# Eight of eleven steps by seven products in the first pair of column blocks of each half

## The chip, the cores and the metric

The kernel runs on one core of a Trainium2 chip. The metric is the device time of one execution in microseconds. Before the change it is 1205.45 us, the median of three runs (1204.93 to 1205.78).

The core's engines run side by side and wait for each other by semaphores. TensorE (PE) multiplies matrices into PSUM, where this kernel keeps eight tiles of 128 x 512 float32 numbers. VectorE (DVE) and ScalarE (ACT) do elementwise work. GpSimd (POOL) does some more and issues DMAs, and SyncE (SP) issues most DMAs. The program holds one order of instructions for each engine.

## The reference

It is one decoder layer over 16 meta tokens and 256 tokens of width 2048: eight retention heads and four mLSTM heads behind one input projection, an output projection, and then a causal ConvFFN and a last norm. The change lies in the ConvFFN and the last norm:

```python
u = rmsnorm(h, norm_ffn)
up = causal_dwconv(u @ w_up, ffn_conv_w, ffn_conv_b)   # 2048 -> 2 * 5632
gate, val = jnp.split(up, [FFN_DIM], axis=-1)
h = h + (jax.nn.silu(gate) * val) @ w_down             # 5632 -> 2048
return rmsnorm(h, norm_final)[:, N_META:]
```

## The kernel before

**Precision.** Every float32 operand of a large product is split into a high part, which ScalarE rounds (`whi`, a CAST), and a low part, which VectorE subtracts (`wlo`). One product of two tiles is then three matmuls: high by high, low by high, high by low.

**Halves.** The hidden width of 5632 is 44 blocks of 128. They are done in two halves of 22 blocks. A half has an up stage, which makes its 22 gated blocks (tiles `gt`), and a down stage, which multiplies them by `w_down` into the 256 x 2048 output. The down stage runs over the output's four column blocks of 512 in two pairs: `b = 0` (blocks 0 and 1), then `b = 2` (blocks 2 and 3). Within a pair it runs over 11 steps `q`; a step takes two of the 22 hidden blocks.

**Plain steps and steps by seven.** In a pair and a step there are 2 x 2 blocks of activations (two hidden blocks, two halves of the tokens) and 2 x 2 blocks of weights (two hidden blocks, two column blocks). A plain step (`product`, L814) does the eight block products, 24 matmuls of 128 x 512. It loads two weight blocks of 128 x 1024 (`load_step`, L910, and `load_w`, L113), and each wants one cast on ScalarE (L119) and one subtraction on VectorE (L121). A step by seven (`seven`, L830) is Winograd's form of Strassen's scheme: seven block products, 21 matmuls, from sums of blocks. It loads weights into a half of the old `hT` tile (`raw`, two of them in turn), makes three differences of weights on VectorE (`ta` and `tb`, L842 and L843), and splits seven blocks in four pieces (L853, through `split`, L764 and L766). The matmuls of a step by seven are L857, L858 and L860. One weight sum of it is made ahead in the up stage by `Early` (L600): GpSimd's queue fetches three weight blocks, VectorE does two operations on them (L616, L617), and GpSimd's queue writes the sum to HBM (`kept`), from where `seven` reads it. `pace` (L609) is a one-column operation of GpSimd's that holds such a fetch back.

**Which steps.** `FAST` lists seven steps, 1, 2, 3, 5, 6, 7 and 8; the other four are `PLAIN`. All pairs do the seven, save the last one (half 1, `b = 2`), where `BOTH`, the steps 7 and 8, are plain; for them the block `a21` is kept split as well. The up stage prepares a fast step's activations in 128 x 128 blocks and four sums of them, which GpSimd makes (L802 to L805).

**What ends a pair.** The four plain sums of a pair (PSUM tiles `atps`, in the code `cs`) and the four shared products of the steps by seven (PSUM tiles `mmps`, in the code `ps`) are put together by VectorE: `share` (L878; L883, L884, L888 and L892) and then four additions (L950). Each addition frees one `atps` bank for the next pair, whose first plain products want it.

**Buffers and order.** Weights come into four buffers `wraw`, which `ta` and `tb` use too; `whi` and `wlo` have five buffers each. The order on each engine is written by a scheduler that models the time of each instruction, from the order of the code and its priorities. The names `x_5852` and `x_5851` in its rows are the tile `x5`, on which `share` and the additions work.

**Small tiles.** `ss4`, `pace`, `rest`, `fr0` and `frt` hold sums of squares and scales of the last norm, and one pacing column. They stand in a pool of their own. `par` holds all parameter columns; those named `cw`, 32 columns, are the mLSTM's convolution weights, which nothing reads once the heads are done.

## Time and profile before

| | |
|---|---|
| Median of three runs | 1205.45 us |
| The profiled execution | 1205.27 us |
| Its span, first to last instruction | 1203.4 us |
| TensorE busy | 1194.6 us, 99% of the span |
| VectorE busy | 978.2 us, 81% |
| ScalarE busy | 704.2 us, 59% |
| GpSimd busy | 156.2 us, 13% |
| Matmuls | 8956 |

The profiled execution took 1.9 us more than its span, which is the time around the first and the last instruction. Busy time says how long an engine had an instruction in work, not how well it used it: matmuls overlap, so the time that one costs is read from one start to the next. The same holds for VectorE, whose instructions overlap by a little. In half 0 the down stage's first pair begins at 717.9 us and its second at 773.65 us, in half 1 at 1082.5 us and 1138.1 us.

### The profile page before, as it was taken

The numbers are of one execution on the slowest core, as the hardware profiler recorded it, in microseconds if no ns is written. First come the engines' busy times: TensorE is split into PE (matmuls) and PEld (weight loads), VectorE is DVE, ScalarE is ACT, GpSimd is POOL, SyncE is SP. The second block draws the span as 40 slices with busy tenths as digits, with TensorE's granted clock in tenths as the row PEclk, the third lists the DMA queues.
The fourth block names the chain that finished last, engine by engine and source line by source line (L and its number), as shares of the span: only waits on it lengthen the run. The fifth ranks groups of instructions, "written<-read, shape, count | busy, mean of one in ns | idle before, by whom it ended". The sixth has DMA issues, their size and how long they took to land.

```text
span 1203.4 us, 22768 instructions
## 1 busy us (share of the span) xinstructions
PE 1194.6 (99%) x8956; PEld 1152.1 (96%) x8956; DVE 978.2 (81%) x1458; ACT 704.2 (59%) x952; POOL 156.2 (13%) x210
## 2 busy tenths in 40 slices
PE   9999999999999999999999999999999999999997
PEld 9999999999999999999999998888999999998886
DVE  8868787766775867788989889998788778789997
ACT  8757656655656556555555556565555555556564
POOL 0100001111110311121112100101122112100131
PEclk9999999999999999999999999999999999999999
DMA  7765555566565965766866734658777677755756
GB/s 279 266 215 165 171 181 172 197 182 196 167 193 161 339 212 181 244 215 209 267 211 221 267 136 175 209 211 272 247 260 253 221 244 245 257 178 209 259 167 192
DMA packets 81275, 260.12 MB, mean 216 GB/s; under 512 B 14480, under 2 KB 18704, under 8 KB 81040
## 3 DMA queue, kind: packets, MB, share of 16 engines
q1 hardware_dynamic: 71952, 223.85, 56.3%
q0 software_dynamic: 8640, 33.96, 8.7%
q8 instruction: 70, 1.15, 0.4%
q10 hardware_dynamic: 576, 0.85, 0.2%
q14 instruction: 37, 0.30, 0.1%
HBM read 243.42 MB, written 11.27 MB: 212 GB/s over the span
## 4 chain that ended last, share of the span: by engine, by line
PE 99%; DMA 0%; SPq 0%; DVE 0%; ACT 0%; issue 0%; DVEq 0%; ACTq 0%
PE mmps L128 26%; PE mmps L129 25%; PE mmps L131 25%; PE atps L828 8%; PE mmps L858 2%; PE mmps L860 2%; PE mmps L857 2%; PE atps L858 1%; PE atps L860 1%; PE atps L857 1%; PE atps L380 1%; PE atps L372 0%; DMA wraw<-in_w 0%; PE atps L128 0%; PE atps L381 0%; PE atps L131 0%
## 5 line engine op out<-in xcount | busy, mean ns | idle before, releaser
L119 ACT CAST whi<-wraw 128x1024 fp32r<-128x1024 f32 x352 | 369.0, 1050 | 329.5 <-PE mmps L129 221.7
L121 DVE TENSOR_TENSOR wlo<-wraw,whi 128x1024 fp32r<-128x1024 f32 x352 | 432.2, 1231 | 66.5 <-ACT whi L119 63.0
L128 PE MATMUL mmps<-uh,whi 128*128 128x258 f32 x1408 | 346.1, 283 | 0.0
L129 PE MATMUL mmps<-ul,whi 128*128 128x258 f32 x1408 | 346.0, 283 | 0.0
L128 PEld LDWEIGHTS mmps<-uh,whi 128*128 128x128 f32 x1408 | 267.6, 190 | 0.1
L129 PEld LDWEIGHTS mmps<-ul,whi 128*128 128x128 f32 x1408 | 267.1, 190 | 0.1
L128 PE MATMUL mmps<-xh,whi 128*128 128x272 f32 (+2 forms) x864 | 219.9, 288 | 0.0
L129 PE MATMUL mmps<-xl,whi 128*128 128x272 f32 (+2 forms) x864 | 218.4, 286 | 0.0
L131 PE MATMUL mmps<-uh,wlo 128*128 128x258 f32 x1408 | 196.5, 282 | 0.0
L131 PEld LDWEIGHTS mmps<-uh,wlo 128*128 128x128 f32 x1408 | 179.9, 189 | 0.0
L129 PEld LDWEIGHTS mmps<-xl,whi 128*128 128x128 f32 x864 | 163.0, 189 | 0.0
L128 PEld LDWEIGHTS mmps<-xh,whi 128*128 128x128 f32 x864 | 162.6, 188 | 0.1
L131 PE MATMUL mmps<-xh,wlo 128*128 128x272 f32 (+2 forms) x864 | 126.8, 286 | 0.0
L131 PEld LDWEIGHTS mmps<-xh,wlo 128*128 128x128 f32 x864 | 114.4, 188 | 0.0
L681 DVE TENSOR_TENSOR cu<-mmps,rstd 128x258 f32<-128x258 f32 x88 | 37.4, 425 | 51.9 <-PE mmps L131 51.1
L764 ACT CAST whi<-hT 128x1024 fp32r<-128x1024 f32 x52 | 53.5, 1051 | 28.1 <-PE atps L828 8.4
L766 DVE TENSOR_TENSOR wlo<-hT,whi 128x1024 fp32r<-128x1024 f32 x52 | 62.7, 1229 | 4.9 <-ACT whi L764 3.7
L129 PE MATMUL mmps<-mixl,whi 128*128 128x258 f32 x256 | 63.0, 283 | 0.0
L128 PE MATMUL mmps<-mixh,whi 128*128 128x258 f32 x256 | 62.4, 282 | 0.0
L764 ACT CAST whi<-wraw 128x1024 fp32r<-128x1024 f32 (+1 forms) x52 | 42.9, 836 | 25.8 <-PE mmps L858 6.0
L766 DVE TENSOR_TENSOR wlo<-wraw,whi 128x1024 fp32r<-128x1024 f32 (+1 forms) x52 | 51.3, 1015 | 1.1 <-PE mmps L860 0.2
L828 PE MATMUL atps<-whi,ml 128*128 128x512 f32 (+1 forms) x132 | 50.7, 385 | 0.0
(284 smaller groups left out, 1696.7 us busy)
## 6 DMA issues: line engine op xcount, KB each, us to landing
wraw<-in_wu SPq DMA_DIRECT2D x176, 512.0 KB, 4.4
wraw<-in_wi SPq DMA_DIRECT2D x108, 512.0 KB, 4.1
hT<-in_wd SPq DMA_DIRECT2D x26, 768.0 KB, 4.7
wraw<-in_wd SPq DMA_DIRECT2D x36, 512.0 KB, 5.2
wraw<-in_wo SPq DMA_DIRECT2D x32, 512.0 KB, 4.4
x<-in_wd POOLq DMA_DIRECT2D x13, 768.0 KB, 7.2
hT<-kept SPq DMA_DIRECT2D x26, 256.0 KB, 2.7
hT<-in_wd POOLq DMA_DIRECT2D x8, 768.0 KB, 6.1
```

What stands on the lines that cost most here:

```text
L119: nc.scalar.copy(hi, raw)
L121: nc.vector.tensor_tensor(out=lo, in0=raw, in1=hi.bitcast(F32), op=ALU.subtract)
L128: nc.tensor.matmul(ps, hi[:, k, :], xh(kk), start=kk == first, stop=False)
L129: nc.tensor.matmul(ps, hi[:, k, :], xl(kk), start=False, stop=False)
L131: nc.tensor.matmul(ps, lo[:, k, :], xh(kk), start=False, stop=kk == last)
L681: evacuated = nc.vector.tensor_tensor(out=u, in0=ps[:, :NQ], in1=rstd2, op=ALU.mult)
L764: copied = nc.scalar.copy(hi, x)
L766: return copied, nc.vector.tensor_tensor(out=lo, in0=x, in1=hi.bitcast(F32), op=ALU.subtract)
L828: nc.tensor.matmul(ps, a, m[:, i, cols], start=first and n == 0, stop=seed or last and n == 5, skip_group_check=seeded)
L857: nc.tensor.matmul(o, sh[:, f, m, :], hi[:, i, :], start=begin, stop=False)
L858: nc.tensor.matmul(o, sl[:, f, m, :], hi[:, i, :], start=False, stop=False)
L860: nc.tensor.matmul(o, sh[:, f, m, :], lo[:, i, :], start=False, stop=end)
```

## The change

`FAST` gets an eighth step, 9, so `PLAIN` is left with 0, 4 and 10. A table `SEVEN` says which fast steps go by seven products in which pair: all eight in the first pair of each half, seven in the second pair of half 0 (9 stays plain there), and the same five as before (1, 2, 3, 5 and 6) in the last pair. `BOTH` names by half the steps that are plain in its second pair, and whose `a21` block is kept. `Early` makes two sums more, one in each half. To make room in SBUF, the small tiles of the last norm and `pace` move into columns of `cw`, and the tile `vt` of the up stage has one buffer in place of two.

```diff
-    FAST = [1, 2, 3, 5, 6, 7, 8]
+    FAST = [1, 2, 3, 5, 6, 7, 8, 9]
     PLAIN = [q for q in range(NQD) if q not in FAST]
-    BOTH = FAST[-2:]
+    BOTH = {0: [9], 1: [7, 8, 9]}
+    SEVEN = {(0, 0): FAST, (0, 2): FAST[:-1], (1, 0): FAST, (1, 2): FAST[:-3]}
...
-    ss4 = midp.tile([P, 2, 5], F32, name="ss4")
+    ss4 = pcol("cw", 0, 10).rearrange("p (t i) -> p t i", t=2)
...
-    pace = midp.tile([P, 1], F32, name="pace")
+    pace = pcol("cw", 10)
...
-        o = wk2.tile([P, SEQ], F32, name=name)
+        o = wk2.tile([P, SEQ], F32, name=name, bufs=2 if name == "gt" else 1)
...
-    rest = midp.tile([P, 2], F32, name="rest")
-    r0 = midp.tile([P, 2], F32, name="fr0")
-    rt = midp.tile([P, 2], F32, name="frt")
+    rest, r0, rt = (pcol("cw", 11 + 2 * i, 2) for i in range(3))
...
-        units = [(b, q) for b in (0, 2) for q in FAST if (half, b) != (1, 2) or q not in BOTH]
+        units = [(b, q) for b in (0, 2) for q in SEVEN[half, b]]
...
-            begins = [2 + 4 * i for i in range(9)]
-            homes = 9 * [homes[2]]
+            begins = [2 + 4 * i for i in range(10)]
+            homes = 10 * [homes[2]]
...
-                if half == 1 and q in BOTH:
-                    split(*(a[:, BOTH.index(q), :] for a in a21), e21)
+                if q in BOTH[half]:
+                    split(*(a[BOTH[half].index(q)] for a in a21), e21)
...
-            fast = [q for q in steps if q in FAST and not (final and q in BOTH)]
+            fast = [q for q in steps if q in SEVEN[half, b]]
```

The order moves on VectorE where the first pair of a half ends. These are the rows of before there, in half 0: they begin with the two low parts of the weights of step 9, and end with the first two of the four additions (L950).

```order
L121 TENSOR_TENSOR wlo<-wraw,whi 128x1024 x2
L883 TENSOR_TENSOR x_5852<-mmps,x_5852 128x512
L884 TENSOR_TENSOR x_5852<-mmps,x_5852 128x512
L888 TENSOR_TENSOR x_5852<-x_5852,mmps 128x512
L892 TENSOR_TENSOR x_5852<-x_5852,mmps 128x512
L121 TENSOR_TENSOR wlo<-wraw,whi 128x1024
L842 TENSOR_TENSOR wraw<-hT 128x1024
L121 TENSOR_TENSOR wlo<-wraw,whi 128x1024 x2
L843 TENSOR_TENSOR wraw<-hT 128x512
L950 TENSOR_TENSOR x_5852<-atps,x_5852 128x512
L121 TENSOR_TENSOR wlo<-wraw,whi 128x1024
L950 TENSOR_TENSOR x_5852<-atps,x_5852 128x512
```

The four operations of `share` (L883 to L892) stand together, well ahead of the first addition, and only one difference of the next pair (L842, L843) stands between. The same place in the changed program, where all line numbers are lower by one; the two low parts at the head are those of step 10, for step 9 has none:

```order
L121 TENSOR_TENSOR wlo<-wraw,whi 128x1024 x2
L882 TENSOR_TENSOR x_5851<-mmps,x_5851 128x512
L841 TENSOR_TENSOR wraw<-hT 128x1024
L842 TENSOR_TENSOR wraw<-hT 128x512
L883 TENSOR_TENSOR x_5851<-mmps,x_5851 128x512
L949 TENSOR_TENSOR x_5851<-atps,x_5851 128x512
L121 TENSOR_TENSOR wlo<-wraw,whi 128x1024
L887 TENSOR_TENSOR x_5851<-x_5851,mmps 128x512
L891 TENSOR_TENSOR x_5851<-x_5851,mmps 128x512
L121 TENSOR_TENSOR wlo<-wraw,whi 128x1024
L841 TENSOR_TENSOR wraw<-hT 128x1024
L949 TENSOR_TENSOR x_5851<-atps,x_5851 128x512 x3
```

`share` is now spread out (L882, L883, L887, L891), the first addition stands in the middle of it, and a whole pair of differences for the next pair (L841, L842) and a third wide one (L841) stand ahead of the other three additions. In half 1 the rows of before are those of half 0 but for the last one, which is three additions. Those of the change there, from the first low part of step 10 on:

```order
L121 TENSOR_TENSOR wlo<-wraw,whi 128x1024
L882 TENSOR_TENSOR x_5851<-mmps,x_5851 128x512
L121 TENSOR_TENSOR wlo<-wraw,whi 128x1024
L841 TENSOR_TENSOR wraw<-hT 128x1024
L883 TENSOR_TENSOR x_5851<-mmps,x_5851 128x512
L842 TENSOR_TENSOR wraw<-hT 128x512
L949 TENSOR_TENSOR x_5851<-atps,x_5851 128x512
L887 TENSOR_TENSOR x_5851<-x_5851,mmps 128x512
L891 TENSOR_TENSOR x_5851<-x_5851,mmps 128x512
L121 TENSOR_TENSOR wlo<-wraw,whi 128x1024 x2
L949 TENSOR_TENSOR x_5851<-atps,x_5851 128x512 x3
```

Here the low part of the next pair's first weights (the first of the two at L121 behind L891) stands behind the first addition and both last operations of `share`; in half 0 it stands between the first addition and those.

## Rows read from the trace of the kernel before

**Rows 1.** The page's head: span; busy time, share and instructions of each engine

```profile
span 1203.4 us, 22768 instructions
PE 1194.6 (99%) x8956; PEld 1152.1 (96%) x8956; DVE 978.2 (81%) x1458; ACT 704.2 (59%) x952; POOL 156.2 (13%) x210
```

**Rows 2.** The page's chain that ended last, share of the span by engine

```profile
PE 99%; DMA 0%; SPq 0%; DVE 0%; ACT 0%; issue 0%; DVEq 0%; ACTq 0%
```

**Rows 3.** Busy time of each engine in three stretches; first line names the columns

```profile
core 0: us, PE busy (x) PEld busy (x) DVE busy (x) ACT busy (x) POOL busy (x), PEclk, DMA share, GB/s
717.00:774.00 57.00, 57.00 (x254) 46.68 (x254) 51.25 (x56) 36.32 (x40) 0.19 (x1) 1.00 0.56 203
...
829.00:1082.00 253.00, 253.00 (x2109) 252.82 (x2108) 200.93 (x300) 136.59 (x184) 41.84 (x68) 1.00 0.72 242
1082.00:1138.00 56.00, 56.00 (x249) 46.05 (x248) 52.16 (x58) 37.48 (x42) 1.33 (x2) 1.00 0.65 231
```

**Rows 4.** Timeline, TensorE, first pair of half 0: its begin and end

```profile
start us, us, engine line op out<-in xcount [idle before <-releaser]
717.89 0.39 PE L828 MATMUL atps<-whi,mh 128*128 128x512 f32 x1
718.12 0.39 PE L828 MATMUL atps<-whi,ml 128*128 128x512 f32 x1
...
772.60 1.07 PE L828 MATMUL atps<-wlo,mh 128*128 128x512 f32 x4
773.65 0.47 PE L828 MATMUL atps<-whi,mh 128*128 128x512 f32 x1
```

**Rows 5.** Timeline, VectorE: last steps by seven of that pair, and an addition

```profile
749.34 1.82 DVE L766 TENSOR_TENSOR wlo<-wraw,whi 128x1024 fp32r<-128x1024 f32 x2
751.08 2.35 DVE L766 TENSOR_TENSOR wlo<-hT,whi 128x1024 fp32r<-128x1024 f32 x2
753.35 1.22 DVE L842 TENSOR_TENSOR wraw<-hT 128x1024 f32<-128x1024 f32 x1
754.48 0.68 DVE L843 TENSOR_TENSOR wraw<-hT 128x512 f32<-128x512 f32 x1
755.09 1.82 DVE L766 TENSOR_TENSOR wlo<-wraw,whi 128x1024 fp32r<-128x1024 f32 x2
...
759.09 1.82 DVE L766 TENSOR_TENSOR wlo<-wraw,whi 128x1024 fp32r<-128x1024 f32 x2
...
772.82 0.68 DVE L950 TENSOR_TENSOR x<-atps,x 128x512 f32<-128x512 f32 x1
```

**Rows 6.** Timeline, TensorE: where it uses the piece that VectorE makes from 759.09

```profile
762.75 0.62 PE L860 MATMUL mmps<-wlo,sh 128*128 128x512 f32 x2
```

**Rows 7.** Groups of VectorE instructions by form, 718 to 829 us

```profile
L766 DVE TENSOR_TENSOR wlo<-hT,whi 128x1024 fp32r<-128x1024 f32 x26 | 31.0, 1219 | 1.7 <-ACT whi L764 1.7
L843 DVE TENSOR_TENSOR wraw<-hT 128x512 f32<-128x512 f32 x12 | 8.2, 684 | 0.0
L950 DVE TENSOR_TENSOR x<-atps,x 128x512 f32<-128x512 f32 x5 | 3.3, 684 | 0.0
```

**Rows 8.** Timeline, ScalarE: casts of plain steps' weights and what they waited for

```profile
766.46 1.05 ACT L119 CAST whi<-wraw 128x1024 fp32r<-128x1024 f32 x1 [2.84 <-DMA wraw<-in_wd]
767.73 1.05 ACT L119 CAST whi<-wraw 128x1024 fp32r<-128x1024 f32 x1 [0.22 <-DMA wraw<-in_wd]
...
770.31 1.05 ACT L119 CAST whi<-wraw 128x1024 fp32r<-128x1024 f32 x1 [0.23 <-DMA wraw<-in_wd]
```

**Rows 9.** Timeline, half 1: VectorE at 1118, TensorE at the second pair's begin

```profile
1118.74 1.82 DVE L766 TENSOR_TENSOR wlo<-wraw,whi 128x1024 fp32r<-128x1024 f32 x2
...
1138.13 0.39 PE L828 MATMUL atps<-whi,mh 128*128 128x512 f32 x1
```

**Rows 10.** Groups of VectorE and GpSimd instructions, 480 to 717 us

```profile
L616 DVE TENSOR_TENSOR x<-x 128x512 f32<-128x512 f32 x9 | 6.2, 688 | 4.0 <-DMA x<-in_wd 4.0
...
L804 POOL TENSOR_TENSOR x<-x,gt 128x128 f32<-128x128 f32 x7 | 6.8, 967 | 0.6
```

More of the change, by code (lines that the diff above doesn't have):

```diff
@@ L760, in trunk @@
         sl = midp.tile([P, len(FAST), 7, P], F32R, name="sl")
-        a21 = [midp.tile([P, len(BOTH), P], F32R, name=n) for n in ("a21h", "a21l")]
+        a21 = [[m[:, i, :] for i in range(3)] for m in [midp.tile([P, 3, P], F32R, name=n) for n in ("a21h", "a21l")]]
         def split(hi, lo, x, after=None):
@@ L823, in product @@
                 f = FAST.index(q)
-                ah, al = ([m[:, f, A12 if i else A11, :] if tt == 0 else m[:, f, A22, :] if i else a[:, BOTH.index(q), :] for i in range(2)]
+                ah, al = ([m[:, f, A12 if i else A11, :] if tt == 0 else m[:, f, A22, :] if i else a[BOTH[half].index(q)] for i in range(2)]
                           for m, a in zip((sh, sl), a21))
```

## The prediction

> **What bounds the kernel now.** I read the page's head first: TensorE is busy 99% of the span and VectorE 81% [rows 1]. The chain that ended last agrees: 99% of it is TensorE [rows 2]. So what shortens TensorE's own work shortens the kernel, and what makes TensorE wait lengthens it, with no slack on either side. The stages come next. In the first pair of each down stage TensorE is busy all the time at a granted clock of 1.00, that is 2.4 GHz, but VectorE is busy 51.25 of 57 us in half 0 and 52.16 of 56 us in half 1, 90% and 93%, well over its 81% of the whole [rows 3]. The change adds VectorE work exactly there. The timelines then give the rates. One 128 x 512 matmul follows another after 0.228 us (717.89 to 718.12, and four of them from 772.60 make 773.51); the pair takes 7 x 21 + 4 x 24 = 243 of them, from 717.89 to 773.65, that is 55.76 us or 0.2295 each, with one stall of 0.14 us in it, at 773.51 [rows 4]. Else TensorE keeps its pace throughout.
>
> **What is removed.** A plain step costs TensorE 24 matmuls and a step by seven 21. One step changes its kind in the first pair of half 0 and one in that of half 1; the other pairs keep seven and five. That is 6 matmuls fewer, 6 x 0.2286 = 1.37 us, all on the path that sets the end. The 0.14 us at 773.51 belong to the place that I work out below, so they leave the sum there too. Together 1.51 us can be won at most.
>
> **What is added, on VectorE.** A step by seven costs VectorE four wide operations (1024 columns) and two narrow ones (512). From 749.34 to 755.09 one such step follows another with no idle time, so it takes 5.75 us; in these rows a wide one costs 1.135 us start to start (two from 751.08 to 753.35) and a narrow one 0.60 us (754.48 to 755.09) [rows 5]. The mean durations, 1.219 and 0.684 us, are longer because neighbours overlap [rows 7]. TensorE's share of the step is 21 x 0.2286 = 4.80 us. So in a run of such steps VectorE falls behind by 0.95 us a step, and catches up in plain ones: two wide operations, 2.27 us, against 24 x 0.2286 = 5.49 us. Before, the run is 5, 6, 7, 8, and 9 and 10 are there to catch up. Now 9 belongs to the run, and only 10 is left before the pair's end, where `share` and the four additions come due.
>
> How far ahead is VectorE? The last wide piece of the run in half 0 is made from 759.09 to 760.31; TensorE takes it at 762.75 [rows 5, 6]. That is 2.4 us of lead. Up to 759.09 the change moves nothing in that pair, so I go on from there in the order of the changed program. From there to the second of the four additions stand 11 wide operations (the first piece at 759.09, one difference of step 9 and its three wide pieces, the two low parts of step 10, two wide differences of the next pair, and the two low parts of its first step) and 9 narrow ones (a piece of step 8, the narrow difference and piece of step 9, one narrow difference of the next pair, the four of `share`, and the first addition). 759.09 + 11 x 1.135 + 9 x 0.60 = 776.98; the addition takes 0.684 us [rows 7] and ends at 777.66. On it waits the first product of the next pair into the bank that it empties. TensorE comes there at 773.51 - 3 x 0.2286 + 16 x 0.2286 = 776.48: the pair is three matmuls shorter, and 16 of the next pair stand ahead. The hand-over takes 0.15 us: before, the first addition ran from 772.82 for 0.68 us, and the product that waited for it started at 773.65 [rows 4, 5]. So TensorE waits 777.66 + 0.15 - 776.48 = 1.3 us.
>
> This holds if nothing else delays VectorE on the way. One thing may. Four buffers go round, so the first weight block of the next pair now lands in the one that step 9's wide difference leaves. Before, the block that came three loads behind a run's last wide difference was cast at 766.46 after a wait for its DMA, and that buffer had been free since 760.31: 6.15 us [rows 5, 8]. Now the low part that reads that difference last has four wide and two narrow operations ahead of it: 759.09 + 4 x 1.135 + 2 x 0.60 + 1.22 = 766.05. The cast then starts at 772.2 and ends at 773.25. VectorE's slot for its low part would be 759.09 + 8 x 1.135 + 7 x 0.60 = 772.37, so everything behind slips by 0.9 us. TensorE wants the cast at 772.82 and the low part four matmuls later, and loses 0.45 us at the one and 0.5 at the other; the wait at the addition shrinks as much as it slips and stays 1.3 us. That makes 2.2 us. So half 0 loses 1.3 to 2.2 us.
>
> In half 1 the same place is ordered otherwise. From 1118.74 [rows 9] 11 wide and 7 narrow operations lead to the first addition, at 1135.43, but that one has to wait for its own bank, whose last product starts seven matmuls before the pair's end at 1138.13 - 0.69 = 1137.44 and takes 0.39 us: 1136.23. Behind it stand two operations of `share`, and then the low part that the next pair's fifth matmul wants: 1136.23 + 3 x 0.60 + 1.22 = 1139.25, with the hand-over 1139.4. TensorE comes there at 1137.44 + 4 x 0.2286 = 1138.35 and waits 1.05 us. After that the additions come in time.
>
> **What I cost at nothing.** In the up stages step 9 now wants one split of 128 columns more, four small sums on GpSimd of up to 0.97 us each, and `Early` two VectorE operations of 0.69 us and one more fetch a half [rows 10]. VectorE has 52 us to spare in the 253 us of the second up stage, and GpSimd works 42 of them [rows 3]; TensorE doesn't wait there now. Without that cover it would be some 2 us a half. The one buffer of `vt` is read by a product that ends before the next block pair is half done. The small tiles in `cw` are written and read by the same instructions as before; only their place is new. The tail has no instruction more for it. If a tie to other columns of `par` added waits there, each would cost a hand-over of 0.15 us, for some five operations in a row 0.75 us; a gain I see no reason for.
>
> **The sum.** -1.51 + (1.3 to 2.2) + 1.05 = +0.85 to +1.75 us, in the middle +1.3. On the profiled execution's 1205.27 us that is 1206.6; the median of the runs stands 0.18 us above it, so I predict 1206.8 us. The ends are those of the first half: no delay by the load, or the delay of the row. About 0.2%, 2.4 us, is what a measurement of this kernel can tell from no change, and my forecast lies within it.
>
> **Rivals.**
> - *The gain comes whole* (1205.45 - 1.51 = 1203.9 us). For it speaks that TensorE is the chain and that VectorE's 81% leave room [rows 1, 2]; the lead would have to be 1 to 2 us longer than I count, as it is where a stage's order lets VectorE work ahead. The Trainium skill's "Perfetto Trace Analysis", section "Identifying the Most-Contended Engine", says to find the engine with the highest occupancy and work on that one; by it the change takes work from the right engine and the whole 1.51 us would show. Its measure for TensorE, LDWEIGHTS busy, is 96% here [rows 1], which agrees, but VectorE's 90% in these stages is what the average hides [rows 3].
> - *The loads make it slower* (1209.4 us). Step 9's transfers fall into the burst at the pair's end. Landings there come 1.28 us apart (766.46, 767.73) and casts wait for them [rows 8]. A step by seven fetches 1 MB, twice a plain block, so if it goes ahead of the next pair's weights in one half these are 2 x 1.28 = 2.6 us later, and TensorE with them: 1206.8 + 2.6. It decides from 1.1 us of such delay on, where the bound of 2.4 us over the median is passed. Against it: a block of step 9 can be fetched as soon as step 7 has used its half of `hT`, two steps of 4.80 us earlier.
> - *VectorE's operations don't overlap* (1209.4 us). Had each its full 1.219 or 0.684 us [rows 7], some 0.084 us more, the 20 operations of half 0 would take 1.7 us longer; the 18 of half 1 would take 1.5 us, of which 0.8 are hidden by the wait for the bank, and the three behind it 0.25: 1206.8 + 1.7 + 0.95. The Trainium skill's "VectorE: DVE Perf Modes", section "The DRAIN you can't avoid", says that the next operation doesn't start until the pipe is empty, though it excepts one that isn't held back; by the plain rule this time would come. The trace speaks against it: 1.135 us start to start for operations of 1.22 us [rows 5].
>
> That the step isn't taken off TensorE can't be: the changed program holds six matmuls fewer.
>
> **How the numbers follow.** Forecast 0.48, whole gain 0.26, later loads 0.17, no overlap 0.03, and 0.06 for a shift elsewhere, either way. The forecast and the whole gain lie within 2.4 us, but a gain of 1.5 us with some luck in the order could reach past it (0.04); the slow ones lie beyond. So faster 0.04, same 0.74, slower 0.22. The range goes from 1203.8, the whole gain, to 1208.9, which leaves out the later loads at their full price. The forecast's own range is 1206.3 to 1207.3.
>
> **What would show it.** TensorE's timeline should have 21 matmuls for step 9 in both first pairs. At the begin of the second pair of half 0 a gap of 1 to 2 us should stand before a plain product that waits for an addition of VectorE, and in half 1 one of 1 us before a low part. VectorE should be without idle time for some 20 us ahead of both. If these gaps are not there I am wrong about the lead; if they stand behind a cast that waits for a DMA, the second rival is right; if gaps stand in the up stages or the tail, my noughts are wrong.

## The result, and the profile after

The changed kernel takes 1211.63 us in the median of six runs (1210.63 to 1215.02), the kernel before on the same chip 1205.35 us: a ratio of 1.0058, 95% interval 1.0049 to 1.0068. It is slower by 6.3 us, 0.6%, where I forecast +1.4 and no change that can be told; the measured time lies beyond the upper end of my range, 1208.9. The profiled execution took 1210.63 us, with a span of 1208.7 against 1203.4 us.

The page's head and its chain of waits, which answer to [rows 1, 2]:

```profile
span 1208.7 us, 22809 instructions
PE 1194.6 (99%) x8950; PEld 1148.8 (95%) x8950; DVE 987.2 (82%) x1474; ACT 706.6 (58%) x960; POOL 167.2 (14%) x224
PE 93%; DVE 3%; DMA 2%; issue 1%; ACT 0%; DVEq 0%; SPq 0%; ACTq 0%
```

The six matmuls are gone (8956 to 8950). But the chain, which was TensorE alone, now leads through VectorE and DMAs for 5% of the span. TensorE's timeline says where; these are its rows that begin after idle time in half 0 and half 1 (the bracket says for how long, and what ended it), and the row ahead of the first:

```profile
765.75 0.61 PE L859 MATMUL mmps<-wlo,sh 128*128 128x512 f32 x2
767.28 0.50 PE L827 MATMUL atps<-whi,mh 128*128 128x512 f32 x1 [0.91 <-ACT whi L119]
776.36 0.50 PE L856 MATMUL mmps<-whi,sh 128*128 128x512 f32 x1 [0.22 <-ACT whi L763]
778.75 0.50 PE L827 MATMUL atps<-whi,mh 128*128 128x512 f32 x1 [0.24 <-DVE x L949]
790.29 0.50 PE L856 MATMUL atps<-whi,sh 128*128 128x512 f32 x1 [0.56 <-ACT whi L763]
...
1134.19 0.50 PE L827 MATMUL atps<-whi,mh 128*128 128x512 f32 x1 [0.94 <-ACT whi L119]
1141.40 0.50 PE L827 MATMUL atps<-whi,mh 128*128 128x512 f32 x1 [0.80 <-ACT whi L119]
1143.12 0.73 PE L827 MATMUL atps<-wlo,mh 128*128 128x512 f32 x2 [0.52 <-DVE wlo L121]
1144.55 0.50 PE L856 MATMUL mmps<-whi,sh 128*128 128x512 f32 x1 [0.22 <-ACT whi L763]
1180.39 0.73 PE L859 MATMUL mmps<-wlo,sh 128*128 128x512 f32 x2 [0.62 <-DVE wlo L765]
```

What a wait costs is read start to start: two matmuls from 765.75 would let the next begin at 765.75 + 2 x 0.2286 = 766.21; it began at 767.28, so 1.07 us are lost. Summed in this way over the places that stand out, half 0 lost 1.07 + 0.16 + 0.39 + 0.42 + 0.72 = 2.76 us, half 1 0.14 + 1.11 + 0.96 + 0.69 + 0.39 + 0.78 = 4.07 us. With the 1.37 us won and the 0.14 of before that is +5.3 us, as much as the span grew by. There are no new gaps in the up stages and the tail.

That the sum comes out is partly luck, for it leaves out two things that cancel. It leaves out small losses: 0.27 us in the two matmuls ahead of 775.40, and some 0.1 us each time TensorE starts again behind a wait. With these the waits are 8.4 us. And it leaves out that TensorE's pace changed. In each pair of rows, 50 matmuls lie from the first to the second; before:

```profile
740.09 0.39 PE L828 MATMUL atps<-whi,mh 128*128 128x512 f32 x1
...
751.53 0.39 PE L858 MATMUL mmps<-whi,sl 128*128 128x512 f32 x1
```

After:

```profile
740.14 0.39 PE L827 MATMUL atps<-whi,ml 128*128 128x512 f32 x1
...
751.47 0.39 PE L856 MATMUL atps<-whi,sh 128*128 128x512 f32 x1
```

That is 11.44 us against 11.33, or 0.2288 against 0.2266 us a matmul, at a granted clock of 1.00 in both. The difference runs through both kernels' down stages wherever TensorE doesn't wait. For the some 950 matmuls of this width there it makes about 2.1 us won, an estimate from these rows. So the waits cost more than the 5.3 us by which the span grew: 5.3 + 1.37 + 0.14 + 2.1, some 9 us.

Most of the rows name ScalarE's casts. ScalarE's timeline tells what these waited for; the four of the border in half 0 answer to [rows 8]:

```profile
766.18 1.04 ACT L119 CAST whi<-wraw 128x1024 fp32r<-128x1024 f32 x1 [3.05 <-DMA wraw<-in_wd]
767.65 1.05 ACT L119 CAST whi<-wraw 128x1024 fp32r<-128x1024 f32 x1 [0.42 <-DMA wraw<-in_wd]
...
772.10 1.05 ACT L119 CAST whi<-wraw 128x1024 fp32r<-128x1024 f32 x1 [2.92 <-DMA wraw<-in_wd]
773.36 1.05 ACT L119 CAST whi<-wraw 128x1024 fp32r<-128x1024 f32 x1 [0.21 <-DMA wraw<-in_wd]
```

The first two are step 10's, the others those of the next pair's step 0. VectorE meanwhile did what I had added up from [rows 5], up to 764.84. Then it waited for step 10's casts, 0.60 us at 767.26 and 0.25 us at 768.73, so that the first addition came at 772.81, where the sum gives 771.8. The second began at 778.01. I had worked out 776.98, and 777.9 if the next pair's load delayed VectorE; but the low part of that load, at 773.41, didn't wait.

```profile
759.10 1.22 DVE L765 TENSOR_TENSOR wlo<-wraw,whi 128x1024 fp32r<-128x1024 f32 x1
...
764.84 1.82 DVE L765 TENSOR_TENSOR wlo<-wraw,whi 128x1024 fp32r<-128x1024 f32 x2
767.26 1.23 DVE L121 TENSOR_TENSOR wlo<-wraw,whi 128x1024 fp32r<-128x1024 f32 x1 [0.60 <-ACT whi L119]
...
772.81 0.68 DVE L949 TENSOR_TENSOR x<-atps,x 128x512 f32<-128x512 f32 x1
773.41 1.21 DVE L121 TENSOR_TENSOR wlo<-wraw,whi 128x1024 fp32r<-128x1024 f32 x1
...
778.01 1.88 DVE L949 TENSOR_TENSOR x<-atps,x 128x512 f32<-128x512 f32 x3
```

SP's queue shows when the loads were issued. Before (each pair of `kept` and `in_wd` is the 1 MB of a step by seven, each `wraw` 512 KB of a plain one):

```profile
759.20 0.33 SPq L838 DMA_DIRECT2D hT<-kept  x1
759.59 0.42 SPq L839 DMA_DIRECT2D hT<-in_wd  x1
760.34 4.41 SPq L116 DMA_DIRECT2D wraw<-in_wd  x4
```

After:

```profile
759.21 0.33 SPq L837 DMA_DIRECT2D hT<-kept  x1
759.59 0.41 SPq L838 DMA_DIRECT2D hT<-in_wd  x1
760.34 2.67 SPq L116 DMA_DIRECT2D wraw<-in_wd  x2
764.95 0.33 SPq L837 DMA_DIRECT2D hT<-kept  x1
765.32 0.43 SPq L838 DMA_DIRECT2D hT<-in_wd  x1
766.08 0.93 SPq L116 DMA_DIRECT2D wraw<-in_wd  x2
```

Step 10's weights are issued at 760.34 in both, when VectorE's low part frees their buffer. Before, a plain step lay between the run and step 10; now TensorE wants them right behind the run, and they take 5.74 us (chain of waits). The next pair's weights, issued by 764.75 before, are issued at 766.08. That is when their buffer comes free, for the low part that reads step 9's wide difference ends at 766.06. Just ahead of them in the queue, at 764.95, stands 1 MB of rows of the next pair's step 2 (step 1's are those of 759.21).

### The profile page after: what moved, and what is told of

Its sections match the earlier page's. It is cut to its first block, busy times and chain, and to the rows that moved or that the text cites. A ratio compares the mean times of both kernels' runs of the same rounds, so it can differ in the third digit from the quotient of the medians.

```text
span 1208.7 us, 22809 instructions
## 1 busy us (share of the span) xinstructions
PE 1194.6 (99%) x8950; PEld 1148.8 (95%) x8950; DVE 987.2 (82%) x1474; ACT 706.6 (58%) x960; POOL 167.2 (14%) x224
## 4 chain that ended last, share of the span: by engine, by line
PE 93%; DVE 3%; DMA 2%; issue 1%; ACT 0%; DVEq 0%; SPq 0%; ACTq 0%
PE mmps L128 25%; PE mmps L129 25%; PE mmps L131 25%; PE atps L827 6%; DVE wlo L765 2%; PE mmps L859 1%; PE mmps L856 1%; PE mmps L857 1%; DMA wraw<-in_wd 1%; PE atps L856 1%; PE atps L859 1%; PE atps L857 1%; DMA hT<-in_wd 1%; PE atps L380 1%; PE atps L372 0%
## 5 line engine op out<-in xcount | busy, mean ns | idle before, releaser
L119 ACT CAST whi<-wraw 128x1024 fp32r<-128x1024 f32 x348 | 364.4, 1050 | 332.8 <-PE mmps L129 219.9
L121 DVE TENSOR_TENSOR wlo<-wraw,whi 128x1024 fp32r<-128x1024 f32 x348 | 427.7, 1231 | 69.1 <-ACT whi L119 65.6
L763 ACT CAST whi<-hT 128x1024 fp32r<-128x1024 f32 x56 | 57.2, 1050 | 25.4 <-DMA hT<-in_wd 9.6
L765 DVE TENSOR_TENSOR wlo<-hT,whi 128x1024 fp32r<-128x1024 f32 x56 | 66.4, 1216 | 1.0 <-ACT whi L763 1.0
L763 ACT CAST whi<-wraw 128x1024 fp32r<-128x1024 f32 (+1 forms) x56 | 45.4, 835 | 21.2 <-PE mmps L857 4.6
L129 PEld LDWEIGHTS mmps<-mixl,whi 128*128 128x128 f32 x256 | 48.4, 189 | 0.0
```

The costliest lines, as they stand in the source:

```text
L119: nc.scalar.copy(hi, raw)
L121: nc.vector.tensor_tensor(out=lo, in0=raw, in1=hi.bitcast(F32), op=ALU.subtract)
L129: nc.tensor.matmul(ps, hi[:, k, :], xl(kk), start=False, stop=False)
L763: copied = nc.scalar.copy(hi, x)
L765: return copied, nc.vector.tensor_tensor(out=lo, in0=x, in1=hi.bitcast(F32), op=ALU.subtract)
```

## The experiments

Three explanations stand against each other. Theory A: VectorE's sum is the bound (8 x 5.75 + 3 x 2.27 + 8 x 0.60 = 57.6 us a first pair, where TensorE needs 240 x 0.2267 = 54.4 us). Theory B: the loads make TensorE wait, because the weights' buffers come free late and the transfers take long. Theory C adds to B the weights' place in SP's queue. Each run is compared with the kernel before on the same chip; ratios with 95% intervals.

**All of the change but its step.**

```diff
-    SEVEN = {(0, 0): FAST, (0, 2): FAST[:-1], (1, 0): FAST, (1, 2): FAST[:-3]}
+    SEVEN = {(0, 0): FAST[:-1], (0, 2): FAST[:-1], (1, 0): FAST[:-1], (1, 2): FAST[:-3]}
```

> The change without its step: step 9 stays plain in all four pairs, while the new homes of the small tiles, the single buffer of vt and the sums and splits for step 9 in the up stages stay. The matmuls are those of the kernel before. Both theories (VectorE's sum, the loads) put the loss into the down stages, so both expect the time of before, 1205.3 us, within 0.5. If the up stages, the one buffer of vt or the columns of cw cost something, it stands here, up to the whole 6.3 us.

Measured 1204.88 us, 0.9999 (0.9989 to 1.0008). So the loss comes with the step; by the time, the rest of the change costs nothing, as both theories had it. The profile shows that this is a balance: e1 has the faster pace of the changed kernel (0.2266 us a matmul from 740.17 to 751.50) and no wait in its down stages, and from the first pair's begin to the last matmul it takes 475.56 us, the kernel before 477.43. Of these 1.87 us it gives back 0.5 ahead of the first pair and 0.5 behind the last matmul; in the medians 0.25 are left. So the pace doesn't come from the step, but from something else in the change; which edit it is, no run separates.

**Half 0 alone.** As above, with `(0, 0): FAST`.

> Step 9 by seven only in the first pair of half 0. By the gaps in TensorE's timeline of the changed kernel half 0 lost 2.8 us of new waits and won 0.69 + 0.14, so 1207.3 us if the halves add up, and half 1 would hold the other 4 us. If one half's delay is given on to the other, the two shares don't add up to 6.3.

Measured 1208.49 us, 1.0027 (1.0016 to 1.0038): +3.4 us, a little over half of the 6.3, so by difference half 1 holds 2.9. By its gaps alone half 0 should have had 2.0; its profile shows the same places with somewhat longer waits (1.61 us before step 10).

**The narrow difference on GpSimd.**

```diff
-            nc.vector.tensor_tensor(out=tb[:, 0, :], in0=raw[:, 3, :], ...
+            nc.gpsimd.tensor_tensor(out=tb[:, 0, :], in0=raw[:, 3, :], ...
```

> The changed kernel with the narrow difference of every step by seven (512 columns) on GpSimd. Theory A, VectorE's sum: a first pair asks 8 x 5.75 + 3 x 2.27 + 8 x 0.60 = 57.6 us of VectorE and 54.4 of TensorE, so VectorE is late and everything that waits for it too. 8 x 0.60 = 4.8 us less make it 52.8, the waits go, and the gain of the six matmuls shows: 1203.9 us. Theory B, the loads: the weights of step 10 come 5.8 us after their buffer is free, behind the 1 MB of step 9; its buffer hangs on low parts that come a little earlier, so the cast of step 10 still waits, some 1 us in each half: 1208 to 1210 us. A third outcome: GpSimd slows VectorE's operations beside it (their mean above 1.22 us), and the time stays or rises.

Measured 1231.54 us, 1.0220 (1.0206 to 1.0234): the third outcome. GpSimd's and VectorE's timelines, side by side:

```profile
739.78 2.03 POOL L842 TENSOR_TENSOR wraw<-hT 128x512 f32<-128x512 f32 x1 [2.57 <-DMA hT<-in_wd]
```

```profile
739.42 1.22 DVE L765 TENSOR_TENSOR wlo<-hT,whi 128x1024 fp32r<-128x1024 f32 x1
740.56 2.32 DVE L841 TENSOR_TENSOR wraw<-hT 128x1024 f32<-128x1024 f32 x1
742.81 1.21 DVE L765 TENSOR_TENSOR wlo<-hT,whi 128x1024 fp32r<-128x1024 f32 x1
```

The operation takes GpSimd 2.03 us where VectorE needs 0.68, and the VectorE operation beside it 2.32 us instead of 1.22. VectorE loses more (1.1) than it is spared (0.60). The test says nothing on A or B.

**Step 9 without its transfers**, `if q != FAST[-1]:` ahead of the two loads of `raw`.

> The changed kernel without the two transfers of step 9 (1 MB) in both first pairs: step 9 takes step 7's rows, which are still there, so its part of the output is another; all work of the engines is as in the changed kernel. Theory B, the loads: step 10's first block then lands some 2.6 us earlier, the gaps of 1.07 and 1.11 us before it go, and with them part of what follows: 1207 to 1209 us. Theory A, VectorE's sum: VectorE has as much to do as ever, the wait only changes its name, from the cast to a low part or an addition of VectorE: 1211 us, within 1.

Measured 1214.61 us, 1.0086 (1.0073 to 1.0099), and inconclusive: in SP's queue the 1 MB of the next pair's step moved into the free place (761.23) and step 10's weights were issued later (762.97). I had tested the queue's order without holding it.

**The narrow difference in x5**, so that a step by seven takes one weight buffer, not two.

```diff
-            ta, tb = (wpool.tile([P, 2, 512], F32, name="wraw", bufs=4) for _ in range(2))
+            ta = wpool.tile([P, 2, 512], F32, name="wraw", bufs=4)
+            k = 1 if turn else 3
+            tb = x5[:, k : k + 1, :]
```

> The changed kernel with the narrow difference of each step by seven in two tiles of x5, which lie idle between the shares, instead of in a weight buffer. VectorE does the same work; a step by seven then takes one of the four weight buffers instead of two, so the buffers for step 10 and for the next pair's first weights come free a step or more earlier. Theory B (the loads wait for buffers): the gaps behind casts that wait for a DMA of wraw, 1.07 us in half 0 and 1.11 + 0.96 in half 1, go, and what stays is what VectorE's sum gives at the pair's end, my forecast's 1.3 + 1.05: 1206 to 1208 us. Theory A (VectorE's sum of 57.6 us against TensorE's 54.4 is the cause, the buffers are only where it shows): the gaps move to low parts and additions, 1210 to 1212 us.

Measured 1213.22 us, 1.0056 (1.0042 to 1.0070). Step 10's casts no longer made TensorE wait at 766; the next pair's weights, issued behind another 1 MB, did, for 2.94 us from 774.9 on. B's edit alone doesn't help.

**Less work for VectorE in the first pairs**, copies for both differences.

```diff
-            nc.vector.tensor_tensor(out=ta, in0=raw[:, 0:1, :]..., in1=raw[:, 1:3, :], op=ALU.subtract)
-            nc.vector.tensor_tensor(out=tb[:, 0, :], in0=raw[:, 3, :], in1=raw[:, 0, :], op=ALU.subtract)
+            nc.vector.tensor_copy(out=ta, in_=raw[:, 1:3, :])
+            nc.vector.tensor_copy(out=tb[:, 0, :], in_=raw[:, 3, :])
```

> The changed kernel with copies in place of the two differences of each step by seven in the first pairs (the products then take the rows themselves, so that part of the output is another): same tiles, same waits, same transfers, less time on VectorE if a copy is shorter than a difference. Were it half as long, a step would cost VectorE 0.8 to 0.9 us less, the first pair 6.8 us less, 50.8 against TensorE's 54.4. Theory A: all waits in the down stages go, 1203.9 us. Theory B: the buffers still come late by what the transfers take, but VectorE frees them earlier by the same sum, so at most some 0.5 us a half stays: 1204 to 1205 us. Were a copy as long as a difference: 1211.6 us, and nothing is learned.

Measured 1211.18 us, 1.0043 (1.0030 to 1.0056): 5.1 us over before, where the changed kernel has 6.3, with intervals that overlap. ScalarE's casts at the border of half 0:

```profile
766.47 1.04 ACT L119 CAST whi<-wraw 128x1024 fp32r<-128x1024 f32 x1 [3.98 <-DMA wraw<-in_wd]
...
772.67 1.05 ACT L119 CAST whi<-wraw 128x1024 fp32r<-128x1024 f32 x1 [3.39 <-DMA wraw<-in_wd]
```

VectorE has 0.53 + 0.26 us less to do in each step (copies of 0.69 and 0.42 us), and the loads come when they came. A's edit alone doesn't help either.

**Orders of the first pairs, with x5**: step 4 one place later, then three (`[0, 1, 2, 3, 5, 6, 7, 4, 8, 9, 10]`).

> As e6, with step 4, the plain one in the middle of the first pairs, one place later: runs of four and four instead of three and five steps by seven. By VectorE's lead (0.95 us lost in a step by seven, 3.22 won in a plain one, and no more than the buffers hold) three and five waste some 0.4 us of what the plain step gives: 0.3 to 0.5 us a half faster than e6 if VectorE's lead at the pair's end decides (theory A), the same as e6 if it doesn't.

> As e6, with step 4 three places later: runs of six and two. Before the middle plain step VectorE's lead falls by 6 x 0.95 = 5.7 us. Theory A: if the lead at the pair's begin is under that, a new gap stands before step 4 and the time is over e8's; if it is more, the time is that of e8. Theory B: step 10's buffers come free as in e8, and step 4's weights have to land in the middle of a long run, so one more wait for a cast there, up to 1 us a half.

Measured 1212.42 us, 1.0048 (1.0036 to 1.0060), and 1211.13 us, 1.0045 (1.0030 to 1.0060). The second had but one wait a border, 2.36 and 2.67 us, at the cast of the next pair's step 1, behind a cast that waited for a DMA.

**The queue.** The rows of a second pair's first two steps by seven behind its step 0's weights; alone, with x5, and with both orders.

```diff
+            with tc.issue_after(last_load.ins) if b and q < 3 else nullcontext():
                 nc.sync.dma_start(raw[:, 0, :], early[b, q])
                 nc.sync.dma_start(raw[:, 1:4, :], ...)
```

> The changed kernel with one edit in SP's queue: the rows of the first two steps by seven of a second pair (1 MB each) are issued behind the weights of its plain step 0, which TensorE wants first. In the changed kernel 1 MB of such rows (issued at 764.95) stood ahead of those weights (issued at 766.08, cast at 772.10), in the kernel before the weights went from 762 on without it and were cast at 769.02. Theory C (place in the queue): the weights of step 0 land about 3 us earlier, the waits at 775 to 778 and at 1140 to 1143 go or shrink to what VectorE's additions give, the wait before step 10 (1.07 and 1.11 us) stays: 1208 to 1209.5 us. Theory A (VectorE's sum): nothing changes, 1211 us within 1.

> f1 and the narrow differences in x5, so that the four weight buffers come free earlier as well. Theory C: now neither the buffers nor the queue delay step 10's or the next pair's weights: no gap of 1 us or more is left in half 0, what stays is what my forecast named, VectorE at the additions: 1206 to 1207.5 us; with VectorE in time even there, 1204. Theory A: 1211 us.

> f2 with step 4 one place later, runs of four and four steps by seven. The smallest gaps at the pair's end of all variants, if VectorE's lead there counts 0.35 us a half: 0 to 0.7 us faster than f2. If it gains, 1203.9 to 1206 us, it beats the kernel before or equals it.

> f2 with step 4 three places later, runs of six and two. Step 10's weights follow a run of two, so their buffers and VectorE are earliest here; the long run is in the middle. Without the queue edit this order lost 2.36 and 2.67 us, all at the first cast of the next pair's step by seven, behind a cast that waited for a DMA: theory C says that these go: 1204 to 1206 us. Theory A: over 1209 us.

Measured 1213.53, 1212.62, 1213.78 and 1210.18 us; 1.0062 (1.0050 to 1.0074), 1.0060 (1.0047 to 1.0073), 1.0076 (1.0062 to 1.0090), 1.0045 (1.0033 to 1.0057). The expectations were missed. The place in the queue does count: in f1 the first block of the next pair was cast 3.6 us after its issue (766.81 to 770.40), in the changed kernel 6.0 us (766.08 to 772.10). But now the rows of step 1, wanted before the second weight block, came late: TensorE waited 3.01 us at 775.49 in f3 and 2.16 us at 1139.31 in f4 for a cast of them.

And f2 shows what stands behind the loads. Step 10 is in time there, and what TensorE waits for at the two borders is the first of VectorE's additions. My forecast had such waits for VectorE, of 1.3 us at the second addition in half 0 and of 1.05 us at a low part in half 1:

```profile
773.61 0.47 PE L827 MATMUL atps<-whi,mh 128*128 128x512 f32 x1 [1.44 <-DVE x L952]
...
1139.74 0.47 PE L827 MATMUL atps<-whi,mh 128*128 128x512 f32 x1 [0.87 <-DVE x L952]
```

In half 0 VectorE had worked up to that addition from 754.66 with 0.2 us of idle time. In f4 two steps by seven run ahead of step 10, not five. Its stretches show a first pair in half 0 with eight steps by seven and no wait of TensorE, and at the border behind it no gap of 0.2 us either:

```profile
717.00:772.00 55.00, 55.00 (x247) 45.59 (x247) 53.62 (x61) 36.73 (x43) 0.00 (x1) 1.00 0.60 209
```

**Rows between the weight blocks**, step 4 three places later, x5 in the first pairs only; and the same in half 0 alone.

```diff
+            with tc.issue_after(loads[begun + q - 1].ins) if b and q < 3 else nullcontext():
                 nc.sync.dma_start(raw[:, 0, :], early[b, q])
...
+            tb = wpool.tile([P, 2, 512], F32, name="wraw", bufs=4) if b else x5[:, k : k + 1, :]
```

> The changed kernel with step 4 three places later in the first pairs (as f4), the narrow differences in x5 in the first pairs only, and the rows of the next pair's step 1 issued between the two weight blocks of its step 0, step 2's behind both. In f4 the first pair of half 0 had TensorE busy all of 717 to 772 us with eight steps by seven, with VectorE busy 53.62 of these 55; what remained there were 0.93 us for x5's tiles in the second pair, and in half 1 2.32 us for step 1's rows, which stood behind a weight block whose buffer was late. Theory C (buffers and places in the queue): these go, half 0 is without a gap over 0.5 us, the last pair keeps about 1 us: 1204 to 1206 us. Theory A (VectorE's sum): the waits come back elsewhere, 1209 us or more.

> f5's edits in half 0 alone, and half 1 as in the kernel before with its seven steps by seven (but for the sums of step 9 in its up stage). Theory C: half 0 wins its 0.69 + 0.14 us, half 1 has no new wait: 1204.6 us, 0.9993 of before. Theory A: 1206.5 us or more.

Measured 1207.94 us, 1.0023 (1.0014 to 1.0032), and 1206.30 us, 1.0005 (0.9996 to 1.0014). Buffers, order and queue together give back 3.5 of the 6.3 us; at half 1's border 0.26 us are left of 3.29. f6 can't be told from the kernel before.

**The last pair without GpSimd's multiplications** (the output lacks the factor `gfin` there), in the changed kernel.

> The changed kernel without the four multiplications by gfin that GpSimd does beside the last pair's steps by seven (so the output lacks that factor there); orders of the other engines and of the queue are unchanged. In the changed kernel a VectorE operation beside such a one, of 2.28 us, took 1.1 us longer (two in 2.91 us at 1178.02 instead of 1.82). If that is what the last pair loses, the gap of 0.78 us at 1179 goes and the time is 0.8 us less than the changed kernel's; everything up to 1150 us stays as it was. If the gap stays, it is the delay that the pair brought along from its begin.

Measured 1211.55 us, 1.0053 (1.0036 to 1.0070). The gap at 1179 is gone, and none is left behind 1150 us. VectorE in the changed kernel, then without the multiplications:

```profile
1178.02 2.91 DVE L765 TENSOR_TENSOR wlo<-wraw,whi 128x1024 fp32r<-128x1024 f32 x2
```

```profile
1178.01 1.81 DVE L765 TENSOR_TENSOR wlo<-wraw,whi 128x1024 fp32r<-128x1024 f32 x2
```

The time stayed. In the profile the border of half 1 lost 2.04 us at 1140 instead of 0.96: the same transfers, landing later.

**What is left of f5**: f5 with copies for the differences in all pairs, and f5 without GpSimd's multiplications.

> f5 with copies in place of the two differences in all steps by seven (the products take the rows themselves, so the output is another): the queue's order is that of f5, VectorE's work is 0.53 + 0.27 us less in each step. f5 is still 2.8 us over the kernel before and 4.2 us over what six matmuls fewer would give. If this rest is VectorE's work (what remains of theory A), it goes now: 1204 us. If it is transfers and their queue alone, it stays: 1207 to 1208 us.

> f5 without GpSimd's four multiplications by gfin beside the last pair's steps by seven (the output lacks that factor there). In f5's profile the last pair and the tail had some 2.5 us of TensorE's waits in gaps of 0.2 to 0.6 us. If GpSimd's work beside VectorE's makes the last pair late, as in f7, these go: 1205 to 1206 us, 2 us under f5. If not: 1208 us.

Measured 1201.28 us, 0.9965 (0.9952 to 0.9977), and 1204.95 us, 1.0000 (0.9991 to 1.0009). In f8 TensorE has no wait at all from 717 us on, in the first pairs or the last:

```profile
717.00:774.00 57.00, 57.00 (x256) 47.32 (x256) 53.59 (x69) 38.77 (x44) 1.31 (x2) 1.00 0.60 208
1082.00:1138.00 56.00, 56.00 (x248) 46.36 (x247) 52.23 (x64) 37.98 (x41) 3.51 (x4) 1.00 0.73 244
1138.00:1190.00 52.00, 52.00 (x247) 43.66 (x246) 44.89 (x55) 31.73 (x45) 13.89 (x13) 1.00 0.57 168
```

Its loads could be issued early (SP's queue; this is the next pair's first block, issued at 766.08 in the changed kernel):

```profile
756.78 0.33 SPq L116 DMA_DIRECT2D wraw<-in_wd  x1
```

SP's queue has the same order in f5 and f8. But f8 is 4.4 us under the kernel before, of which the six matmuls and the wait of [rows 4] explain 1.5. So the last run put the same copies into the kernel before.

> The kernel before with copies in place of the two differences of all its steps by seven (the output is another). f8 came out at 0.9965 of before, 4.4 us, of which six matmuls and the wait of before explain 1.5. If the copies, by sparing VectorE, take away small waits that the kernel before has in most executions, they do it here too: 1202.5 to 1203 us, and f8's eighth step is worth its 1.5 us on top. If the kernel before has nothing to win from them, 1205.3 us, f8's rest stays unexplained.

Measured 1210.21 us, 1.0039 (1.0026 to 1.0053): slower by 5.1 us, which neither side expected. In its profile TensorE waits 2.31 us behind 794.09, in a pair that had no wait, for a cast that waits for its DMA, and then works at a granted clock of 0.62 from 797 to 801:

```profile
795.53 1.04 ACT L119 CAST whi<-wraw 128x1024 fp32r<-128x1024 f32 x1 [5.40 <-DMA wraw<-in_wd]
```

The scheduler had written a new order: SP's queue is the same as before, but 411 of TensorE's 8956 matmuls stand at another place, counted by the tiles in the two traces; between f5 and f8 it is 512 of 8950, between the changed kernel and e7 295. So a shorter VectorE operation isn't the only thing that these edits change, and e7, f8 and g1 don't measure VectorE's work alone. What f8 shows is that the eight steps by seven can run without a wait. Most of the 2.8 us by which it is better than they explain is the pace: 50 matmuls take 11.34 us in f8 (740.00 to 751.34), as in the changed kernel, and the estimate of 2.1 us holds for it too. g1, made from the kernel before, has that kernel's pace (0.229 us), so it couldn't show this. Some 0.7 us stay open.

What the runs settle: the loss comes with the step and lies in the down stages (e1). At the borders of the pairs casts wait for weights that were issued late or behind other rows (the trace, f1's 6.0 and 3.6 us, and f5, whose edits aim at just that). With the loads in time, VectorE's additions are late next (f2), unless the order of the steps gives it time (f4). In the last pair GpSimd's multiplications cost something: f9, whose order of matmuls is f5's, gives back all of the 2.8 us that f5 has over the kernel before. Theory A in its plain form, 57.6 us of VectorE in 54.4, is wrong: f4's first pair ran all eight with VectorE busy 53.62 of 55 us and no wait. But VectorE is not out of it, as f2 shows. What f9 still lacks of the gain are waits in half 0, the longest 1.14 us at 773.76; how much of them is VectorE's work and how much the order stays open.

## Why the prediction was wrong

**Six matmuls, 1.37 us.** Right: there are 8950 matmuls, and in f8, where nothing waits, the kernel is faster than before.

**What I cost at nothing.** Right by e1's time, but partly by luck. I took 0.2286 us a matmul for both kernels; the change made it 0.2267, some 2.1 us that no term of mine has. In e1 half of them are lost again outside the down stages; in the changed kernel they hide a part of the waits.

**VectorE's sum.** In half 0 right to a tenth of a microsecond up to 764.84. That 777.9 for the second addition nearly came true (778.01) is luck: VectorE was held up by step 10's casts, which I had not counted, and not by the next pair's load, which I had. The wait at that addition was there, 0.42 us behind 778.10 instead of 1.3, because TensorE itself came late by then. f2 shows such a wait at full size. In half 1 the sum began from a row that moved. The piece that VectorE made at 1118.74 before [rows 9] is this one after:

```profile
1122.62 1.82 DVE L765 TENSOR_TENSOR wlo<-wraw,whi 128x1024 fp32r<-128x1024 f32 x2
```

It comes 3.88 us later, and the pair's begin only 2.0 us (1084.52 against 1082.51). So VectorE's lead in half 1 was 1.9 us smaller than I took it to be.

**The load at the next pair's begin.** Right: the buffer worked out to come free at 766.05, the load issued at 766.08; the cast worked out for 772.2 from the 6.15 us of [rows 5, 8], made at 772.10. Instead of the 0.95 us that it was to cost, 0.16, 0.27 and 0.39 us are lost at the pair's begin.

**The step that failed** is "So half 0 loses 1.3 to 2.2 us", and with it half 1's 1.05. I used those 6.15 us once, for the next pair's first block, and not for the block to which the row itself belongs. The cast at 766.46 in [rows 8] is step 10's; the change doesn't move it, but brings TensorE to it at 766.21 instead of 768. That is 1.07 us in half 0, in plain sight. The 1.11 us at the same place in half 1 come from the smaller lead: the load took 3.5 us there from issue to cast (1129.62 to 1133.09), but VectorE's low part had freed its buffer only at 1129.59. Nor did I take the price of a load to the rows of the next steps by seven (0.72 us at 789) or through half 1 at all, where I worked out a low part and no load: 1.11 + 0.96 + 0.69 + 0.39 us stand there instead of 1.05 (the 0.69 are that low part). And the last pair, 0.78 us, I had no term for; in f7, without GpSimd's multiplications, that gap is gone. The range of 1.3 to 2.2 us and the 1.05 us together allowed 3.25 us of waits at the most, and the changed kernel has 8.4.

**The rivals.** "The loads make it slower" was nearest: its mechanism, a step's 1 MB ahead of the next pair's weights, is the 764.95 in SP's queue, and without it, in f1, the block was cast 2.4 us sooner after its issue, near the 2.6 us of the rival. My reason against it (the rows of step 9 can be fetched early) was true, they are issued at 753.46, but of the wrong step: it is the next pair's step 2 that stands ahead. I gave it 0.17, for one half. Waits for step 10's own load it didn't have either. "The gain comes whole" failed. By the Trainium skill's "Perfetto Trace Analysis", section "Identifying the Most-Contended Engine", the engine with the highest occupancy is the one to optimize first. TensorE is still that engine, but here taking work from it at VectorE's and the buffers' cost made the kernel slower. "VectorE's operations don't overlap" failed: 759.10 to 764.84 has six operations of the expected spacing, four wide and two narrow.

## What to carry to other kernels

Where an engine is busy 99%, list for each load of the stretch that a change touches when its buffer comes free, what stands ahead of it in the queue, and when its reader wants it; a price read off one load is to be tried on all of its kind. (It is no constant: in the changed kernel alone these loads took 3.5 to 6.7 us from issue to cast, the longest from 1133.62 to 1140.30.) Where a scheduler writes the orders, an edit that only shortens an operation moves hundreds of other instructions too: compare the orders before a time is put down to the operation, and prefer edits that keep them (f7, f9). A sum of waits that matches the time isn't proof that it is whole: compare the pace between the waits as well. A step that spares the bound engine 3 matmuls (0.69 us) and costs the next one 3.48 us is worth it only where that engine and the buffers have so much to spare.

## What the runs showed of the hardware

**GpSimd beside VectorE.** In e3 GpSimd's operation ran from 739.78 to 741.81; the VectorE operation that began at 740.56 ended at 742.88, 1.07 us after it, nearly its own 1.22 us. So it looks as if VectorE stood still until GpSimd was done. The Trainium skill's "SBUF — State Buffer", section "Who interferes with whom", says that the two share a pair of ports as an exclusive lock, and that a VectorE instruction with two SBUF inputs contends for it with a GpSimd instruction that reads SBUF; these rows agree. Without the four such multiplications of the last pair f5 is some 3 us faster (f9).

**TensorE's pace.** With a granted clock of 1.00 and no wait, a matmul of 128 x 512 follows another after 0.2288 us in the kernel before and in g1, and after 0.2267 us in the changed kernel and in all its variants that I looked at, e1 among them. What in the change does it is not shown.

**TensorE's clock after a long wait.** In e6 TensorE stood still for 2.94 us from 774.9 on, and then worked at a granted clock of 0.51, about 1.2 GHz, up to 784. Stretches (the last three columns are the clock, the DMA share and GB/s), then TensorE's rows:

```profile
777.00:780.00 3.00, 2.16 (x5) 1.78 (x6) 3.00 (x6) 1.74 (x2) 0.92 (x1) 0.51 0.24 43
784.00:790.00 6.00, 6.00 (x28) 4.94 (x27) 3.89 (x6) 2.75 (x4) 0.00 (x0) 1.00 0.82 200
```

```profile
778.86 0.63 PE L858 MATMUL mmps<-whi,sh 128*128 128x512 f32 x1
779.28 0.63 PE L859 MATMUL mmps<-whi,sl 128*128 128x512 f32 x1
```

A matmul costs 0.42 us there, not 0.227; the fourteen that start from 777.84 to 783.55 take 6.1 us, 2.9 more than at that pace. That profile is of e6's slowest execution, 1215.78 us.

**Spread.** The six runs of the kernel before in the first comparison lie within 1.4 us, those of the changed one between 1210.6 and 1215.0. In the profile of f7, whose instructions are those of the changed kernel up to the last pair, step 10's weights were cast 5.26 us after their issue (759.52 to 764.78), in the changed kernel's own 5.84 (760.34 to 766.18), and half 1's border lost 1.08 us more at 1140. Where TensorE waits for the load, such a difference goes into the time. That the runs near 1215 are ones in which the clock fell after a wait, as in e6, is likely and not shown.
